# Newton rounds of two reciprocal square roots moved from VectorE to GpSimd in a streaming encoder layer

## The chip, the cores and the metric

The kernel runs on one core of a Trainium2 chip. The metric is the device time of one execution in microseconds (us). The core has five engines that work at the same time and take their own instructions in order: TensorE (PE, matrix products and transposes; PEld are its weight loads), VectorE (DVE), ScalarE (ACT), GpSimd (POOL) and SyncE (SP), which here issues the DMAs. Where an engine needs a result of another one (or, here, where DVE or POOL needs its own earlier result), the instruction waits on a semaphore, and what stands behind it on that engine waits too.

## The reference

One inference step of one hybrid layer for 1024 prompt tokens and 8 x 16 sample tokens, width 1024. The parts that matter here, cut:

```python
h = rmsnorm(x, g_norm)
proj = h @ w_in                                    # 81 groups of 128 columns
r, k, v, w_lr, a_lr, z_a = split(token_shift_mix(proj[..., :SHIFT_COLS]))
kap_h = (k * k_removal).reshape(B, T, 16, 64)
kh_h = kap_h / maximum(norm(kap_h, axis=-1), 1e-12)          # first reciprocal root
y, S = wkv7_scan(wkv0, r_h, w_h, kh_h, a_h, v_h, kt_h)       # recurrence, one state per head
mu = mean(y, -1); var = mean(square(y - mu), -1)
yn = (y - mu) * lax.rsqrt(var + GN_EPS)                      # second reciprocal root
out_a = ((yn * gn_w + gn_b + bonus) * silu(z_a)) @ w_o_a
out_b = (gb * causal_conv3(gc * xb) * silu(z_b)) @ w_o_b
x = x + (sigmoid(g_a) * out_a + sigmoid(g_b) * out_b) @ w_out
x = x + sigmoid(rmsnorm(x, g_ple) @ w_ple_gate) * (p @ w_ple)
y = rmsnorm(x, g_final)
```

## The kernel before

Tokens lie in three blocks: 0 (512 prompt tokens), 1 (the 128 sample tokens) and 2 (the other 512 prompt tokens). The work has three stages. The prologue normalises `x` and transposes it. The recurrence goes through 8 pairs of heads, each with the 3 blocks: 24 steps, named by pair and block, so that `yc4_0` is the `yc` of pair 4, block 0. The last stage multiplies by `w_ob`, `w_oa` and `w_out`, adds the layer's embedding and norms again.

The recurrence is written as seven streams of Python generators. `prep` projects `k`, `r`, `v`, `z` and makes the keys; `scores`, `values` and `inverse` prepare the chunks of 64 tokens; `chain` carries the state `sbd` from chunk to chunk; `tail` makes the output `y`, normalises it per head and writes it to `oa_d`; `conv` is the other branch, whose large matmuls fill gaps. The function `go()` lays these streams into one order on PE: it counts estimated PE time, resumes a stream when the delay that it yielded (`yield 11.0`, in us) has passed, and puts dense matmuls between. That order on PE is fixed. The order on DVE, ACT and POOL isn't written by hand: the tile framework's scheduler lists the instructions by its own estimate of when each can run.

A reciprocal square root is made by `rsqrt`: a seed from the bits of the float (line 134), and three Newton rounds of three instructions (lines 137 to 139), on tiles of 128 partitions by at most 8 columns. It is called

- in `prologue` (5 calls) and in `rstd_rows` for the norms of the last stage (8 calls);
- in `prep` (24 calls, result `nrk`): PE sums squares into `pss`, line 405 copies them to `ssm`, `rsqrt` follows, and ACT spreads the result over 64 columns as `rnb` (line 408). After the products of `v`, PE transposes `rnb` into `prn`, and line 421 scales `k` with it;
- in `tail` (24 calls, result `nry`): the variance `yvr` (lines 705, 706), `rsqrt`, then line 708 multiplies `yc` with it. PE transposes `yc` into `py`, and lines 715, 716 finish the block, which a DMA of SP's queue writes.

Other names that come up: `bdgt` (line 583 on ACT; also line 599 on DVE) and `bdtn` (lines 560, 561 on DVE) are operands of the matmuls that invert a chunk's triangular matrix; `tt`, `tn` (lines 584, 588) are its running inverse; `gt` (line 578) is ACT's copy of one step of it; `xs` (line 643), `vu` (line 649) and `sbd` (line 654) belong to the state's chain; `Spt` (line 638) is POOL's share in it; `thd` (line 362), `zb` (line 768) and `pt` (line 372) are other work of POOL; `wlo...` (line 149) are weight splits.

Of the kernel before, what the change touches and what calls it, by code (L numbers as in the profile page):

```python
# [14 lines left out]
ALU = mybir.AluOpType  # L15
# [56 lines left out]
def _build(nc, tc, I, O, top):  # L72
    V, A, G, PE, SP = nc.vector, nc.scalar, nc.gpsimd, nc.tensor, nc.sync
# [54 lines left out]
        V.tensor_scalar(out=half[:, n, :], in0=par[:, o:o + 8], scalar1=0.5, scalar2=None, op0=ALU.mult)  # L128
    V.tensor_scalar(out=half[:, 3, :], in0=half[:, 2, :], scalar1=-1.0, scalar2=1.0, op0=ALU.mult, op1=ALU.add)

    def rsqrt(x, n, tag):
        y = small.tile([128, 8], F32, tag="nr", name="nr" + tag, bufs=4)[:, :n]
        a = small.tile([128, 8], F32, tag="na", name="na" + tag)[:, :n]
        V.tensor_scalar(out=y.bitcast(I32), in0=x.bitcast(I32), scalar1=-0.5, scalar2=float(0x5F3759DF),
                        op0=ALU.mult, op1=ALU.add)
        for _ in range(3):
            V.tensor_tensor(out=a, in0=y, in1=x, op=ALU.mult)
            V.scalar_tensor_tensor(out=a, in0=a, scalar=-0.5, in1=y, op0=ALU.mult, op1=ALU.mult)
            V.scalar_tensor_tensor(out=y, in0=a, scalar=1.5, in1=y, op0=ALU.add, op1=ALU.mult)
        return y  # L140

    def load_w(src, nm):
# [176 lines left out]
    def load_q(j, q):  # L319
        s = pair(j)  # L320
        if q not in s.w:
            t = {"k": T_K, "r": T_R, "v": T_V, "z": T_ZA}[q]
            s.w[q] = load_w(I["w_in"][t + j], f"p{j}_{t}")
# [17 lines left out]
    def prep(f):  # L341
# [8 lines left out]
        smp, nch, npr, nm = f.smp, f.nch, f.npr, f.nm  # L350
        th = []
        for q, hb in (("d", 0), ("a", 1)):
# [13 lines left out]
                             op0=ALU.mult, op1=ALU.add)  # L366
# [11 lines left out]
        for q, t in (("k", T_K), ("r", T_R), ("v", T_V), ("z", T_ZA)):  # L378
            load_q(j, q)
            if q == "v":  # L380
                yield lambda: S_tail.at >= f.i - 2
            ps = yield from dense_parts(s.w[q], blk, q + nm)
            if ahead:
                load_q(j + 1, q)
            if q == "v":
                x = f.v = tt(wk, "v", "v" + nm, 3, RN)[:, :n]
            elif q == "z":
                x = f.zs = tt(wk, "zs", "zs" + nm, 3, RN)[:, :n]
            else:
                x = tt(st_, "ta", q + nm, TA)[:, :n]  # L390
            mu = (zmu[:, i, j:j + 1] for i in range(3)) if q == "z" else (
                P("mu", t + j), mum[:, t + j:t + j + 1], mus[:, t + j:t + j + 1])
            mixed(ps, t + j, blk, x, *mu, q + nm)
            m[q] = x
            if q == "r":
                x = m["k"]
                yield 4.0

                sq = tt(st_, "ta", "sq" + nm, TA)[:, :n]
                A.activation(sq, x, AF.Square, scale=P("krem", j))  # L400
                pss = psa.tile([128, 512], F32, tag="a", name="pss" + nm)
                for i in range(npr):
                    mm(pss[:, 2 * i:2 * i + 2], sq[:, i * 128:(i + 1) * 128], onesb[:, 0:128:64], start=True, stop=True)
                ssm = small.tile([128, 8], F32, tag="ssm", name="ssm" + nm)
                V.tensor_scalar(out=ssm[:, :2 * npr], in0=pss[:, :2 * npr], scalar1=1e-24, scalar2=None, op0=ALU.max)
                rn = rsqrt(ssm[:, :2 * npr], 2 * npr, "k%d" % npr)
                rnb = tt(st_, "ta", "rnb" + nm, TA)[:, :n]
                A.activation(rnb.rearrange("p (q t) -> p q t", t=64), rn.unsqueeze(2).to_broadcast([128, 2 * npr, 64]),
                             AF.Copy)
            if q == "v":  # L410

                k = m["k"]
                yield 3.0
                prn = psa.tile([128, 512], F32, tag="a", name="prn" + nm)
                for i in range(npr):
                    tr(prn[:, i * 128:(i + 1) * 128], rnb[:, i * 128:(i + 1) * 128], ident)
                kt = tt(st_, "ta", "kt" + nm, TA)[:, :n]
                V.tensor_scalar(out=kt, in0=tha, scalar1=half[:, 2, j:j + 1], scalar2=half[:, 3, j:j + 1],
                                op0=ALU.mult, op1=ALU.add)
                V.tensor_tensor(out=kt, in0=kt, in1=k, op=ALU.mult)  # L420
                V.scalar_tensor_tensor(out=k, in0=k, scalar=P("krem", j), in1=prn[:, :n], op0=ALU.mult, op1=ALU.mult)
                V.scalar_tensor_tensor(out=tha, in0=tha, scalar=1.0, in1=k, op0=ALU.add, op1=ALU.mult)
# [236 lines left out]
    def tail(f):  # L659

        j, s = f.j, f.s
        blk = o, n = f.blk
        smp, nch, npr, nm = f.smp, f.nch, f.npr, f.nm
        nu = 2 * npr
        W = nu * 64
        vu, kbt, pt, scy, yst, bv, zs = f.vu, f.kbt, f.pt, f.scy, f.yst, f.bv, f.zs
        yield 1.0
        yps = psa.tile([128, 4, 2, 64], F32, tag="a", name="y" + nm)[:, :npr]
        for p in range(npr):
            for h, H in enumerate(HS):  # L670
                for e in range(2):
                    mm(yps[HS[e], p, h, :], scy[:, h, p, e, :], vu[:, 2 * p + e, H], start=True, stop=True)
        f.y_done = not smp
        if o + n == 1024:
            for h, H in enumerate(HS):
                SP.dma_start(O["wkv_p"][j, H], sbd[f.st][H, H])
        if smp:
            sst = s.sst
            sso = tt(wk, "ty", "sso" + nm, 2, RN).rearrange("p (s v) -> p s v", v=64)
            for c in range(2):  # L680
                vux = tt(wk, "ty", f"vux{nm}_{c}", 2, RN).rearrange("p (s v) -> p s v", v=128)
                G.tensor_tensor(out=vux, in0=vu[:, c, :].unsqueeze(1).to_broadcast([128, 4, 128]),
                                in1=seq4.unsqueeze(2).to_broadcast([128, 4, 128]), op=ALU.mult)
                yield 1.5
                pS = psc.tile([128, 4, 64], F32, tag="c", name=f"pS{nm}_{c}")
                for h, H in enumerate(HS):
                    mm(pS[H], kbt[:, c, H], vux[:, :, H], start=True, stop=True)
                V.tensor_tensor(out=sso[:, 4 * c:4 * c + 4, :], in0=sst[:, 4 * c:4 * c + 4, :], in1=pS, op=ALU.add)
            f.y_done = True
            V.tensor_tensor(out=sso, in0=sso, in1=pt.unsqueeze(2).to_broadcast([128, 8, 64]), op=ALU.mult)  # L690
            SP.dma_start(O["wkv_s"][j], sso)


        yw = yps.rearrange("p c h v -> p (c h) v")
        y = tt(wk, "ty", "yc" + nm, 2, RN)[:, :W].rearrange("p (u v) -> p u v", v=64)
        ysm = small.tile([128, 8], F32, tag="ysm", name="ysm" + nm)[:, :nu]
        V.tensor_tensor(out=y, in0=yst.rearrange("p c (h v) -> p (c h) v", h=2), in1=yw, op=ALU.add)
        V.tensor_reduce(out=ysm, in_=y, op=ALU.add, axis=AX.X)
        V.tensor_scalar(out=ysm, in0=ysm, scalar1=1.0 / 64, scalar2=None, op0=ALU.mult)
        bcu = lambda x: x.unsqueeze(2).to_broadcast([128, nu, 64])  # L700
        V.tensor_tensor(out=y, in0=y, in1=bcu(ysm), op=ALU.subtract)
        y2 = tt(wk, "ty", "y2" + nm, 2, RN)[:, :W].rearrange("p (u v) -> p u v", v=64)
        A.activation(y2, y, AF.Square)
        yvr = small.tile([128, 8], F32, tag="yvr", name="yvr" + nm)[:, :nu]
        V.tensor_reduce(out=yvr, in_=y2, op=ALU.add, axis=AX.X)
        V.tensor_scalar(out=yvr, in0=yvr, scalar1=1.0 / 64, scalar2=GN_EPS, op0=ALU.mult, op1=ALU.add)
        yrs = rsqrt(yvr, nu, "y%d" % nu)
        V.tensor_tensor(out=y, in0=y, in1=bcu(yrs), op=ALU.mult)
        yf = y.rearrange("p u v -> p (u v)")
        yield 11.0  # L710
        py = psa.tile([128, 512], F32, tag="a", name="py" + nm)
        for i in range(npr):
            tr(py[:, i * 128:(i + 1) * 128], yf[:, i * 128:(i + 1) * 128], ident)
        oa = yf[:, :n]
        V.scalar_tensor_tensor(out=oa, in0=py[:, :n], scalar=P("gnw", j), in1=bv, op0=ALU.mult, op1=ALU.add)
        V.scalar_tensor_tensor(out=oa, in0=oa, scalar=P("gnb", j), in1=zs, op0=ALU.add, op1=ALU.mult)
        SP.dma_start(oa_d[j, :, o:o + n], oa)
# [155 lines left out]
    op = top.enter_context(tc.tile_pool(name="op", bufs=1))  # L873
# [48 lines left out]
    for j in range(KT):  # L922
        w = load_wr(I["w_ob"][j], f"b{j}")
        for blk in BL3:
            o, n = blk
            ps = dense_r(w, obs, blk, f"ob{j}_{o}")
            V.scalar_tensor_tensor(out=ms[j][:, o:o + n], in0=ms[j][:, o:o + n], scalar=1.0, in1=ps,
                                   op0=ALU.add, op1=ALU.mult)
# [11 lines left out]
    for j in range(KT):  # L940
        w = load_wr(I["w_oa"][j], f"a{j}")
        g = gts[j]
        for blk in BL3:
            o, n = blk
# [220 lines left out]
```

## Time and profile before

| | us |
|---|---|
| runs | 1968.08, 1969.87, 1972.9; median 1969.87 |
| the profiled execution, its own time | 1966.13 |
| its span, from the first to the last instruction | 1963.5 |
| PE busy | 1822.7 (93%) |
| DVE busy | 1255.0 (64%) |
| ACT busy | 814.5 (41%) |
| POOL busy | 215.6 (11%) |

The span was recorded in one execution by the profiler. "Busy" is the time in which an engine had an instruction in work; waiting isn't in it. The mean granted clock of PE was 0.984 of full speed.

### The profile page before, as it was taken

What the parts mean: (1) busy time and instruction counts of PE and PEld (TensorE: products, weight loads), DVE (VectorE), ACT (ScalarE), POOL (GpSimd) and SP (SyncE); (2) the same over time, 40 slices, a digit from 0 to 9 for tenths busy, and PEclk for the clock granted to TensorE, in tenths of its full rate; (3) what the DMA queues carried; (4) which work ended last, traced back from release to release, by engine and by line L of the source; (5) the groups of instructions that cost most, each with busy time, mean ns of one, the idle gap of its engine ahead of it and who ended that gap; (6) DMA issues with size and microseconds to landing.
All of it is one profiled execution on the core that took longest, in us unless ns stands there. A gap on an engine that the chain in (4) does not pass through costs nothing. (4 is left out here: it accounts for less than half of the span.)

```text
span 1963.5 us, 37863 instructions
## 1 busy us (share of the span) xinstructions
PE 1822.7 (93%) x15374; PEld 1254.4 (64%) x15374; DVE 1255.0 (64%) x3225; ACT 814.5 (41%) x1877; POOL 215.6 (11%) x333
## 2 busy tenths in 40 slices
PE   4999989989999999999999989889999999999997
PEld 2555666556556556556556556555599677899766
DVE  7477877777687787777887877774223311355665
ACT  6354544544445445445455454443301311322321
POOL 0010121111111111112111111110000011100000
PEclk9999999999999999999999999889999999999999
DMA  6002102101111110201101100022312311243002
GB/s 214 22 23 69 39 14 65 35 28 49 39 40 39 49 40 28 60 29 36 61 28 36 50 8 18 15 69 69 123 42 73 121 44 33 67 123 92 11 29 82
DMA packets 43758, 103.57 MB, mean 53 GB/s; under 512 B 6208, under 2 KB 21440, under 8 KB 43584
## 3 DMA queue, kind: packets, MB, share of 16 engines
q1 hardware_dynamic: 43584, 101.17, 16.2%
q8 instruction: 120, 1.97, 0.4%
q14 instruction: 54, 0.44, 0.1%
HBM read 84.40 MB, written 16.74 MB: 52 GB/s over the span
## 5 line engine op out<-in xcount | busy, mean ns | idle before, releaser
L92 PEld LDWEIGHTS <-whip 128*128 128x128 f16 x1536 | 133.8, 99 | 79.2 <-issue 4.9
L638 POOL TENSOR_SCALAR Spt<-sbd,pt 128x128 f32<-128x128 f32 x128 | 89.8, 702 | 645.1 <-DVE sbd L654 643.8
L92 PEld LDWEIGHTS <-wlop 128*128 128x128 f16 x768 | 75.5, 98 | 61.8 <-issue 2.2
L583 ACT ACTIVATE bdgt<-ig 64x512 f16<-64x512 f32 (+1 forms) x208 | 106.7, 513 | 2.8
L654 DVE SCALAR_TENSOR_TENSOR sbd<-u,pt,Spt 64x64 f32<-64x64 f32 x256 | 72.1, 282 | 52.0 <-PE u L92 44.0
L92 PE MATMUL dB<-hx,whiB 128*128 128x512 f16 (+1 forms) x384 | 91.6, 331 | 3.7 <-ACT sho L236 2.8
L92 PE MATMUL dgb<-hx,whigb 128*128 128x512 f16 (+1 forms) x384 | 91.6, 331 | 2.4 <-ACT whigb L148 1.8
L92 PE MATMUL dzb<-hx,whiZ 128*128 128x512 f16 (+1 forms) x384 | 88.6, 326 | 4.7 <-ACT sho L229 4.7
L644 ACT ACTIVATE yst<-c 64x128 f32<-64x128 f32 x144 | 38.8, 270 | 129.3 <-DVE xs L643 128.1
L92 PE MATMUL dC<-hx,whiC 128*128 128x512 f16 (+1 forms) x384 | 89.9, 327 | 1.5 <-ACT cs L735 1.0
L92 PE MATMUL dv<-hx,whip 128*128 128x512 f16 (+1 forms) x384 | 90.7, 330 | 0.0
L578 ACT ACTIVATE gt<-ig 128x512 f16<-128x512 f32 (+1 forms) x104 | 54.2, 521 | 87.7 <-PE ig L92 87.1
L92 PE MATMUL dk<-hx,whip 128*128 128x512 f16 (+1 forms) x384 | 90.5, 332 | 0.0
L92 PE MATMUL dr<-hx,whip 128*128 128x512 f16 (+1 forms) x384 | 89.0, 326 | 1.4 <-DVE zb L767 1.4
L92 PE MATMUL dz<-hx,whip 128*128 128x512 f16 (+1 forms) x384 | 89.6, 326 | 0.0
L92 PE MATMUL pg<-xn,pg 128*128 128x384 f16 (+1 forms) x576 | 88.9, 309 | 0.0
L92 PE MATMUL dx<-hx,whiX 128*128 128x512 f16 (+1 forms) x384 | 88.3, 326 | 0.5 <-ACT sho L229 0.4
L92 PE MATMUL dga<-hx,whiga 128*128 128x512 f16 (+1 forms) x384 | 86.9, 326 | 0.0
L92 PEld LDWEIGHTS <-pg 128*128 128x128 f16 x768 | 66.3, 99 | 27.1 <-issue 2.4
L649 ACT ACTIVATE vu<-u 64x64 f32<-64x64 f32 x288 | 62.9, 218 | 46.8 <-PE u L92 43.4
L92 PEld LDWEIGHTS u<-xs,tm 128*128 128x128 f32 x288 | 49.9, 191 | 36.8 <-DVE xs L643 21.5
L643 DVE TENSOR_TENSOR xs<-c,vu 64x128 f32<-64x128 f32 x144 | 41.1, 286 | 49.9 <-PE c L92 48.1
(325 smaller groups left out, 4944.1 us busy)
## 6 DMA issues: line engine op xcount, KB each, us to landing
wstp<-i_w_in SPq DMA_DIRECT2D x32, 512.0 KB, 3.6
xt<-i_x SPq DMA_DIRECT2D x9, 512.0 KB, 5.4
ob_d<-zb SPq DMA_DIRECT2D x8, 576.0 KB, 2.9
ostb<-ob_d SPq DMA_DIRECT2D x24, 192.0 KB, 3.0
osta<-oa_d SPq DMA_DIRECT2D x24, 192.0 KB, 2.5
xr<-i_xT SPq DMA_DIRECT2D x8, 576.0 KB, 3.6
wstC<-i_w_in SPq DMA_DIRECT2D x8, 512.0 KB, 3.5
wstX<-i_w_in SPq DMA_DIRECT2D x8, 512.0 KB, 3.5
```

The source lines that it names most:

```text
L92: PE.matmul(out, lhsT, rhs, start=start, stop=stop)
L578: A.activation(Gt, pg, AF.Copy, scale=-1.0)
L583: A.activation(Gb[R, :, R], pg[R], AF.Copy, scale=-1.0)
L638: G.tensor_scalar(out=Spt, in0=S, scalar1=pt[:, c:c + 1], scalar2=None, op0=ALU.mult)
L643: V.tensor_tensor(out=xs[Uh, :], in0=pc[Uh, 0:128], in1=vu[Uh, c, :], op=ALU.add)
L644: A.activation(yst[Vh, p, :], pc[Vh, 0:128], AF.Copy)
L649: A.activation(vu[Uh, c, H], pu[H, H], AF.Copy, scale=-1.0)
L654: V.scalar_tensor_tensor(out=S2[H, H], in0=pu[H, 128 + h * 64:192 + h * 64], scalar=pt[H, c:c + 1], in1=Spt[H, H], op0=ALU.mult, op1=ALU.add)
```

## The change

`rsqrt` gets the engine of its rounds as an argument. The calls in `prep` and `tail` give GpSimd (`G`), the others stay on VectorE. The seed stays on VectorE in all. A round has four instructions instead of three, on either engine, since the two that multiply by a scalar and a tensor at once (SCALAR_TENSOR_TENSOR) are taken apart; the arithmetic is the same.

```diff
-    def rsqrt(x, n, tag):
+    def rsqrt(x, n, tag, E=None):
+        E = E or V
...
         V.tensor_scalar(out=y.bitcast(I32), in0=x.bitcast(I32), scalar1=-0.5, scalar2=float(0x5F3759DF),
                         op0=ALU.mult, op1=ALU.add)
         for _ in range(3):
-            V.tensor_tensor(out=a, in0=y, in1=x, op=ALU.mult)
-            V.scalar_tensor_tensor(out=a, in0=a, scalar=-0.5, in1=y, op0=ALU.mult, op1=ALU.mult)
-            V.scalar_tensor_tensor(out=y, in0=a, scalar=1.5, in1=y, op0=ALU.add, op1=ALU.mult)
+            E.tensor_tensor(out=a, in0=y, in1=x, op=ALU.mult)
+            E.tensor_tensor(out=a, in0=a, in1=y, op=ALU.mult)
+            E.tensor_scalar(out=a, in0=a, scalar1=-0.5, scalar2=1.5, op0=ALU.mult, op1=ALU.add)
+            E.tensor_tensor(out=y, in0=a, in1=y, op=ALU.mult)
         return y
...
-                rn = rsqrt(ssm[:, :2 * npr], 2 * npr, "k%d" % npr)
+                rn = rsqrt(ssm[:, :2 * npr], 2 * npr, "k%d" % npr, G)
...
-        yrs = rsqrt(yvr, nu, "y%d" % nu)
+        yrs = rsqrt(yvr, nu, "y%d" % nu, G)
```

The order on PE in the recurrence is almost untouched, but the scheduler lists DVE, ACT and POOL anew. Behind line 143 the new kernel's line numbers are 2 higher (408 becomes 410, 708 becomes 710), and the seed is line 135. Three places of pair 4 follow.

First place, VectorE around `yc4_0`. Before, 18 rounds' instructions of `yc4_0`'s and `rnb5_0`'s roots stand between the seeds and `yc4_0`; these are the last rows:

```order
L643 TENSOR_TENSOR xs1_135<-c4_1_1_10934,vu4_1_10072 64x128
...
L139 SCALAR_TENSOR_TENSOR nry8_10820<-nay8_10821,nry8_10820 128x8
L139 SCALAR_TENSOR_TENSOR nrk4_10886<-nak4_10887,nrk4_10886 128x8
L708 TENSOR_TENSOR yc4_0_10809<-yc4_0_10809,nry8_10820 128x512
L584 COPY_PREDICATED tt4_2_10616<-cph_99,i134_2_10959 128x512
L747 TENSOR_TENSOR u5_512_10974<-cs5_9667,dx5_512_10716 128x512
```

Now, on VectorE:

```order
L135 TENSOR_SCALAR nry8_10916<-yvr4_0_10913 128x8
L135 TENSOR_SCALAR nrk4_10985<-ssm5_0_10983 128x8
L562 COPY bdtn_128<-tn4_2_10711 64x8x64
L563 COPY bdtn_128<-tn4_2_10711 64x8x64
L645 TENSOR_TENSOR xs1_135<-c4_1_1_11036,vu4_1_10165 64x128
L710 TENSOR_TENSOR yc4_0_10905<-yc4_0_10905,nry8_10916 128x512
L420 TENSOR_SCALAR kt5_0_11345<-tha5_0_10637,half_89 128x512
L586 COPY_PREDICATED tt4_2_10712<-cph_99,i134_2_11061 128x512
```

`yc4_0` comes four rows after its seed. The rounds stand on GpSimd, where those of the two roots alternate; here is the first round, behind a `vux` that was there before:

```order
L684 TENSOR_TENSOR vux4_1_0_11143<-vu4_1_10165,cpk_98 128x512
L138 TENSOR_TENSOR nay8_10917<-nry8_10916,yvr4_0_10913 128x8
L138 TENSOR_TENSOR nak4_10986<-nrk4_10985,ssm5_0_10983 128x8
L139 TENSOR_TENSOR nay8_10917<-nay8_10917,nry8_10916 128x8
L139 TENSOR_TENSOR nak4_10986<-nak4_10986,nrk4_10985 128x8
L140 TENSOR_SCALAR nay8_10917<-nay8_10917 128x8
L140 TENSOR_SCALAR nak4_10986<-nak4_10986 128x8
L141 TENSOR_TENSOR nry8_10916<-nay8_10917,nry8_10916 128x8
L141 TENSOR_TENSOR nrk4_10985<-nak4_10986,nrk4_10985 128x8
```

On ScalarE at the same place, before:

```order
L578 ACTIVATE gt34_2_10947<-ig34_2_10938 128x512
L644 ACTIVATE yst4_1_10760<-c4_1_1_10934 64x128
L583 ACTIVATE bdgt_129<-ig34_2_10938 64x8x64 x2
L408 ACTIVATE rnb5_0_10898<-nrk4_10886 128x512
L649 ACTIVATE vu4_1_10072<-u4_1_1_10955 64x64 x2
```

and now:

```order
L646 ACTIVATE yst4_1_10856<-c4_1_1_11036 64x128
L580 ACTIVATE gt34_2_11049<-ig34_2_11040 128x512
L410 ACTIVATE rnb5_0_11000<-nrk4_10985 128x512
L585 ACTIVATE bdgt_129<-ig34_2_11040 64x8x64
L651 ACTIVATE vu4_1_10165<-u4_1_1_11057 64x64 x2
L585 ACTIVATE bdgt_129<-ig34_2_11040 64x8x64
```

`rnb5_0` has moved ahead of both `bdgt` copies.

Second place, VectorE around `yc4_1`, where a `y` root stands alone. Before:

```order
L599 TENSOR_TENSOR bdgt_129<-loit4_2_11168,ie4_2_11187 64x8x64
L138 SCALAR_TENSOR_TENSOR nay2_11108<-nay2_11108,nry2_11107 128x2
L599 TENSOR_TENSOR bdgt_129<-loit4_2_11168,ie4_2_11187 64x8x64
L139 SCALAR_TENSOR_TENSOR nry2_11107<-nay2_11108,nry2_11107 128x2
L767 SCALAR_TENSOR_TENSOR zb5_10981<-thb5_1024_11224,dzb5_1024_11180 128x128
L708 TENSOR_TENSOR yc4_1_11096<-yc4_1_11096,nry2_11107 128x128
```

and now:

```order
L135 TENSOR_SCALAR nry2_11209<-yvr4_1_11206 128x2
L229 SCALAR_TENSOR_TENSOR v5_0_11281<-dv5_0_11188,mus_83,v5_0_11281 128x511
L710 TENSOR_TENSOR yc4_1_11198<-yc4_1_11198,nry2_11209 128x128
L601 TENSOR_TENSOR bdgt_129<-loit4_2_11273,ie4_2_11292 64x8x64 x2
L769 SCALAR_TENSOR_TENSOR zb5_11083<-thb5_1024_11329,dzb5_1024_11285 128x128
```

The two `bdgt` subtractions that stood ahead of `yc4_1` stand behind it.

Third place, ScalarE around `rnb5_1`, where a `k` root stands alone. Before:

```order
L583 ACTIVATE bdgt_129<-ig25_0_11675 64x8x64 x2
L649 ACTIVATE vu4_2_10846<-u4_2_4_11712 64x64 x2
L408 ACTIVATE rnb5_1_11704<-nrk1_11692 128x128
L148 ACTIVATE whiX6_11757<-wstX6_11755 128x1024
L578 ACTIVATE gt35_0_11774<-ig35_0_11765 128x512
```

and now:

```order
L585 ACTIVATE bdgt_129<-ig25_0_11780 64x8x64 x2
L651 ACTIVATE vu4_2_10945<-u4_2_4_11820 64x64
L410 ACTIVATE rnb5_1_11812<-nrk1_11797 128x128
L651 ACTIVATE vu4_2_10945<-u4_2_4_11820 64x64
L150 ACTIVATE whiX6_11865<-wstX6_11863 128x1024
```

`rnb5_1` has moved between the two `vu4_2` copies of one chunk.

## Rows read from the trace of the kernel before

**Rows 1.** The page, busy time, share of the span and instructions of each engine.
```profile
PE 1822.7 (93%) x15374; PEld 1254.4 (64%) x15374; DVE 1255.0 (64%) x3225; ACT 814.5 (41%) x1877; POOL 215.6 (11%) x333
```

**Rows 2.** Windows: stretch, length, busy PE PEld DVE ACT POOL, clock, DMA, GB/s.
```profile
60.00:1360.00 1300.00, 1206.55 (x11565) 755.07 (x11563) 970.18 (x2592) 624.25 (x1508) 186.12 (x294) 0.99 0.12 38
849.00:1003.00 154.00, 142.85 (x1417) 91.15 (x1417) 119.77 (x325) 76.87 (x188) 23.77 (x37) 1.00 0.12 40
```

**Rows 3.** What PE waited for: us in total, times, longest us.
```profile
PE u L92 <- DVE xs L643: 12.7, 10, 2.2
...
PE prq L246 <- DVE nrq L139: 3.1, 3, 2.3
PE py L96 <- DVE yc L708: 2.8, 3, 1.7
```

**Rows 4.** Groups by form on DVE: count | busy us, mean ns | idle before.
```profile
L137 DVE TENSOR_TENSOR nay<-nry,yvr 128x8 f32<-128x8 f32 x48 | 7.8, 162 | 0.7
```

**Rows 5.** Groups by form on POOL.
```profile
L638 POOL TENSOR_SCALAR Spt<-sbd,pt 128x128 f32<-128x128 f32 x128 | 89.8, 702 | 645.1 <-DVE sbd L654 643.8 <-POOL pb L368 0.2
...
L362 POOL TENSOR_SCALAR thd<-thd 128x512 f32<-128x512 f32 x16 | 24.3, 1519 | 100.0 <-ACT thd L359 86.9 <-DVE sbd L654 13.0
L768 POOL TENSOR_TENSOR zb<-zb,cv 128x512 f32<-128x512 f32 x16 | 23.7, 1482 | 79.1 <-DVE zb L767 79.1
...
L372 POOL COPY pt<-pb 128x8 f32<-128x8 f32 x24 | 6.6, 276 | 28.1 <-ACT pb L370 27.8
L362 POOL TENSOR_SCALAR thd<-thd 128x128 f32<-128x128 f32 x8 | 6.2, 772 | 26.5 <-ACT thd L359 26.5
...
L768 POOL TENSOR_TENSOR zb<-zb,cv 128x128 f32<-128x128 f32 x8 | 3.6, 456 | 44.5 <-DVE zb L767 37.1 <-DVE nry L139 7.4
```

**Rows 6.** Timeline of POOL: start us, duration us, instruction.
```profile
304.58 0.21 POOL L618 MEMSET sbd<- 128x128 f32 x1 [0.93 <-PE ie L92]
304.88 0.72 POOL L638 TENSOR_SCALAR Spt<-sbd,pt 128x128 f32<-128x128 f32 x1
```

**Rows 7.** Timeline of DVE, first place.
```profile
851.16 0.49 DVE L134 TENSOR_SCALAR nry<-yvr 128x8 int32<-128x8 int32 x1
851.57 0.16 DVE L134 TENSOR_SCALAR nrk<-ssm 128x8 int32<-128x8 int32 x1
...
854.18 0.69 DVE L708 TENSOR_TENSOR yc<-yc,nry 128x512 f32<-128x512 f32 x1
```

**Rows 8.** Timeline of ACT, first place.
```profile
854.20 1.21 ACT L583 ACTIVATE bdgt<-ig 64x512 f16<-64x512 f32 x2
855.44 0.63 ACT L408 ACTIVATE rnb<-nrk 128x512 f32<-128x512 f32 x1
```

**Rows 9.** Timeline of PE, first place.
```profile
855.53 0.40 PE L92 MATMUL i<-tn,bdgt 128*128 128x64 f16 x8
```

**Rows 10.** Timelines of DVE and PE, second place.
```profile
872.71 0.17 DVE L134 TENSOR_SCALAR nry<-yvr 128x2 int32<-128x2 int32 x1
...
874.70 0.67 DVE L599 TENSOR_TENSOR bdgt<-loit,ie 64x512 f16<-64x512 f16 x1
...
877.99 0.40 PE L92 MATMUL if<-tn,bdgt 128*128 128x64 f16 x8
```

**Rows 11.** Timelines of DVE, ACT and PE, third place.
```profile
909.82 0.17 DVE L134 TENSOR_SCALAR nrk<-ssm 128x2 int32<-128x2 int32 x1
...
911.78 0.31 ACT L408 ACTIVATE rnb<-nrk 128x128 f32<-128x128 f32 x1
...
912.72 0.47 PE L92 MATMUL u<-vu,kbt 128*128 128x128 f32 x2
```

**Rows 12.** The chain that ended last, at the last tail: start us, us, what.
```profile
1356.19 0.18 DVE nry L134
...
1359.25 0.70 DVE yc L708
```

**Rows 13.** One tile's instructions, `bdtn` on DVE: duration ns min/median/max.
```profile
L560 DVE COPY bdtn<-tn x104: 177/280/1350, 117.8 to 1313.6; 64x512 f16<-64x512 f16 x80, 64x128 f16<-64x128 f16 x24
```

## Prediction

> **What bounds the kernel now.** I read the head of the page first: TensorE (PE) is busy for 1822.7 of 1963.5 us, VectorE (DVE) for 1255.0, GpSimd (POOL) for 215.6 [rows 1]. Then the windows: in the recurrence (60 to 1360 us) DVE is busy 970.18 of 1300 us, and in one period of it (849 to 1003 us, one pair of heads, three blocks of tokens) PE is busy 142.85 of 154 us, DVE 119.77 [rows 2]. So PE bounds the recurrence, and it leaves 154 - 142.85 = 11.15 us per period unused. The list of waits shows that these are small waits for DVE and ScalarE (ACT): the largest, `u<-xs`, is 12.7 us in all in ten pieces, `py<-yc` 2.8 us in three [rows 3]. PE takes its work in the fixed order of `go()`, so whatever comes late by more than its slack stops PE. The question is therefore not how much work DVE loses but whether a result that PE needs comes later.
>
> **What the change takes from DVE.** A round is three dependent instructions of about 0.16 us [rows 4], with issue about 0.2 us from start to start: a reciprocal root of nine costs 1.8 us of DVE. 48 of them (24 `k`, 24 `y`) are 86 us of 970, in an engine that is a quarter idle. By itself that is worth a little: PE waits for DVE with perhaps half of its 11.15 us per period.
>
> **What a chain costs on POOL.** No row shows such a small arithmetic operation there, so I bound it. TENSOR_TENSOR takes 1482 ns for 512 and 456 ns for 128 columns [rows 5]: 2.67 ns a column, so 456 - 120 x 2.67 = 136 ns for 8. The nearest real row is the 128x8 COPY `pt`, 276 ns. I take 0.20 us between them. TENSOR_SCALAR with immediate operands, the form of line 140 of the new kernel, takes 1519 ns for 512 and 772 ns for 128 columns [rows 5]: 1.95 ns a column, 540 ns for 8; I take 0.50 us, near to that row, with 0.14 (a TENSOR_TENSOR) and 0.70 us (`Spt`) as ends. A POOL instruction that needs the one before it starts late: the memset of `sbd` ends at 304.79 us, the `Spt` that reads it starts at 304.88 us [rows 6], 0.09 us. All twelve depend in this way. One chain alone is 9 x (0.20 + 0.09) + 3 x (0.50 + 0.09) = 4.4 us, and with a like 0.1 us for each crossing between engines **4.6 us** from the end of the seed (line 134, which stays on DVE) to the reader. By the low ends it is 12 x 0.23 + 0.2 = 3.0 us, by the high ones 9 x 0.366 + 3 x 0.79 + 0.2 = 5.9 us. On DVE it is 1.8 us.
>
> **What stands behind it.** The order printed above decides it: the scheduler moved the readers forward, as if the chain were short. `yc` (line 708) follows its seed on DVE after one or a few instructions, and `rnb` (line 408) stands on ACT ahead of work that PE needs soon. Both engines take instructions in order, so they stand still until POOL is done, with everything behind. I work out three places of one period; the others have the same form.
>
> Place A, `yc4_0` and `rnb5_0`. Seeds start at 851.16 and 851.57 us and `yc` at 854.18 [rows 7]. On POOL the two chains alternate, so one runs in the other's gaps: 9 x 0.29 + 3 x 0.89 = 5.3 us, from 851.75 to 857.05 us. DVE resumes at 857.1, 2.9 us late. ACT's `rnb` goes from 855.44 to about 857.3 us, and two `bdgt` copies, which ran from 854.20, now stand behind it [rows 8], with `vu` between them: 857.3 + 0.63 + 0.6 + 0.45 + 0.6 = 859.6 us. PE reads `bdgt` at 855.53 us [rows 9]: **4.1 us late**. DVE's own 2.9 us lie inside that, since PE then comes to DVE's next result 4.1 us later too.
>
> Place B, `yc4_1`, a `y` alone. The seed starts at 872.71 and ends at 872.88 us [rows 10]; 4.6 us later, at 877.5, `yc` runs (0.3 us), and the two L599 of 0.67 us that stood ahead of it [rows 10] now come behind: 877.5 + 0.3 + 1.3 = 879.1 us. PE's `if` reads them at 877.99 us [rows 10]: **1.2 us late**.
>
> Place C, `rnb5_1`, a `k` alone. The seed ends at 909.99 us, so `rnb` moves from 911.78 to 914.6 us, and one of the two `vu` copies, now behind it, ends at 915.2 us. PE's `u` that reads it started at 912.72 us [rows 11]: **2.5 us late**. The relief counts here: DVE goes on without its 1.8 us, but PE waits for ACT.
>
> Block 2 of the period has one more of B's form and one more of C's (there `rnb` holds up a `gt` copy). A period: 4.1 + 2 x 1.2 + 2 x 2.5 = 11.5 us; eight periods 92 us. Not all stays. Each time that PE stands, DVE and ACT catch up, and a later small wait of PE shrinks; PE has 11.15 us of them per period. If 40% is taken back so, 0.6 x 92 = **55 us** remain. That factor is my choice, between 0.5 (half of those 11.15 us goes) and 1.
>
> **What else moves.** In the calls that stay on DVE a round has four instructions, so a call is 3 x 0.2 = 0.6 us longer. The first prologue call, the three waits of PE for `nrq` (3.1 us) [rows 3] and the last call lie on the path: 5 x 0.6 = 3 us. The others lie under dense matmuls; uncovered, the other eight would cost 5 us. The tail of the last block sets when `oa_d` is written and when the loads behind it in SP's queue start: seed 1356.19, `yc` 1359.25 us [rows 12], with a weight split between, which now comes after. New: 1356.37 + 4.6 = 1361.0, **1.7 us later**. POOL's own late work costs nothing that I can see: the `Spt` that comes up to 3 us late is needed a chunk later, some 6 us on. DMAs are neither added nor removed.
>
> **Sum.** 1966.1 (the profiled execution: span 1963.5 and 2.6 around it) + 55 + 3 + 2 = 2026 us. The median of the runs lies 3.7 us above the profiled one, so 2026 to 2030; I say **2028 us**. Low prices: A 1.6, B 0, C 0.9, a period 3.4, eight times 0.6: 16 us, 1985 us. High prices: 6.6 + 2 x 2.5 + 2 x 3.8 = 19.2 a period, 92 us at 0.6 and 154 us at 1: 2063 to 2125 us. Within 0.3%, about 6 us, a measurement of this kernel can't tell a change from none.
>
> **Rivals.** First, the two engines hinder each other at SBUF. For it: the 64x512 `bdtn` copy, whose median is 280 ns, once took 1350 ns [rows 13]. Against it: in a `y` chain DVE mostly stands still and can't be in the way. If it holds, the high prices do, and DVE's later work is slowed, so less is taken back: 0.8 x 8 x 19.2 = 123 us, 2094 us. The Trainium skill (SBUF — State Buffer, Who interferes with whom) says that a DVE copy in a two-port mode, or a DVE instruction with two SBUF inputs, and a reading POOL instruction exclude each other for a whole instruction. The long `bdtn` copy agrees with that rule. Chance 0.18.
>
> Second, the other side: POOL does the small operations at the low prices or under. Then a chain (3.0 us) is no longer than what passes today from seed to `yc` (3.0 us at A, 3.9 at B), the waits at `yc` vanish, and DVE's freed 86 us tell. If a quarter of PE's unused time goes, 8 x 11.15 / 4 = 22 us less half of that for `rnb`, plus the 3 us of the longer calls: 1966 - 11 + 3 = 1958 us. It decides at about 3 us a chain. Against it: line 140's form has no row under 772 ns. Chance 0.07.
>
> Third, the lateness is taken back entirely, since PE's order leaves some 2 us between `yc` and `py` (it waited there in 3 of 24 calls [rows 3]) and more ahead of `prn` (none of its waits): 1969 us, no change. Against it: the stall doesn't come from `py` or `prn`, but from what stands behind the readers in DVE's and ACT's queues. Chance 0.08.
>
> **Numbers.** The forecast has 0.67, the rivals 0.18, 0.07 and 0.08. Slower by over 0.3%: 0.67 + 0.18 = 0.85; same 0.08; faster 0.07. The range from 1985 (low prices) to 2085 (short of the first rival's centre) leaves out the no-change and faster cases and part of the first rival, about 0.2.
>
> **What would show it.** Right: POOL busy grows by 576 x 0.275 = 158 us (48 chains of 12, by the mid prices); the chain takes 4 to 5 us; among waits, DVE `yc` for POOL `nry` and ACT `rnb` for POOL `nrk` of 2 to 4 us each, together over 60 us; PE waits for `bdgt`, `vu` and `sbd` grow; a period becomes some 7 us longer, and PE's busy time stays. Wrong: a chain under 3 us; waits of DVE and ACT as forecast, yet periods as long as before (then the factor 0.6 is wrong); or a longer time in the stage behind 1404 us, of which I price only 1 or 2 us.

## Result: slower by 4.1%, and the profile after

Four runs of the changed kernel took 2042.14 to 2054.51 us, median **2050.61**; four of the kernel before 1964.53 to 1972.9, median 1968.97. The ratio is 1.0409 (95% interval 1.037 to 1.0449). The forecast was 2028 us in a range from 1985 to 2085.

The head of the page of the changed kernel, against [rows 1]:

```profile
PE 1846.5 (90%) x15374; PEld 1261.8 (62%) x15374; DVE 1205.5 (59%) x2832; ACT 813.0 (40%) x1877; POOL 347.0 (17%) x909
```

The span is 2049.3 us, 85.8 more than before. PE runs the same 15374 instructions, yet is busy for 23.8 us more; the other 62.0 us is time in which PE stands. DVE is relieved by 49.5 us, POOL has 131.4 us more. The next view is the windows, with the columns of [rows 2]; the first line is the recurrence, which now ends some 79 us later, and the second the period from `yc4_0` on, which took 154.3 us before:

```profile
60.00:1439.00 1379.00, 1227.99 (x11569) 762.05 (x11567) 916.93 (x2163) 623.88 (x1510) 310.48 (x870) 0.97 0.11 36
910.50:1075.00 164.50, 148.11 (x1418) 92.39 (x1417) 113.75 (x271) 77.22 (x187) 38.50 (x110) 0.97 0.12 37
```

PE stands in the recurrence for 1379 - 1227.99 = 151.0 us, before for 1300 - 1206.55 = 93.5. So nearly all of the loss arises there: 57.5 us of standing and 21.4 us of busier time. The period is 10 us longer; here about half of that is PE's busy time (148.11 against some 143), over the whole recurrence about a quarter.

The waits (us in total, times, longest) name the two readers:

```profile
ACT rnb L410 <- POOL nrk L141: 68.7, 24, 6.0
DVE yc L710 <- POOL nry L141: 62.8, 24, 4.2
...
PE u L92 <- DVE xs L645: 18.3, 14, 2.2
PE u L92 <- ACT vu L651: 18.1, 15, 5.3
PE i L92 <- ACT gt L580: 17.0, 10, 3.8
...
PE i L92 <- ACT bdgt L585: 10.1, 7, 2.0
...
PE py L96 <- DVE yc L710: 4.7, 2, 2.5
```

and before, for the three of ACT:

```profile
PE u L92 <- ACT vu L649: 5.9, 10, 1.3
...
PE i L92 <- ACT gt L578: 2.5, 4, 0.7
...
PE i L92 <- ACT bdgt L583: 1.1, 3, 0.5
```

All 24 `rnb` and all 24 `yc` wait for POOL, 131.5 us together. PE hardly waits for the roots themselves: for `yc` at `py` it is 4.7 us, and no wait for `rnb` is among its waits at all. It waits for `vu`, `gt` and `bdgt`, ordinary work of ACT that stands behind `rnb` (45.2 us together, 9.5 before), and for `xs` of DVE (18.3 us, 12.7 before [rows 3]).

The first place of the prediction, by the timelines of DVE, POOL, ACT and PE (start us, us, engine, instruction; in brackets how long the engine stood before it and for whom), against [rows 7 to 9]:

```profile
910.94 0.49 DVE L135 TENSOR_SCALAR nry<-yvr 128x8 int32<-128x8 int32 x1
911.35 0.16 DVE L135 TENSOR_SCALAR nrk<-ssm 128x8 int32<-128x8 int32 x1
...
911.51 0.25 POOL L138 TENSOR_TENSOR nay<-nry,yvr 128x8 f32<-128x8 f32 x1
...
914.91 0.19 POOL L140 TENSOR_SCALAR nay<-nay 128x8 f32<-128x8 f32 x1
915.07 0.19 POOL L140 TENSOR_SCALAR nak<-nak 128x8 f32<-128x8 f32 x1
915.23 0.20 POOL L141 TENSOR_TENSOR nry<-nay,nry 128x8 f32<-128x8 f32 x1
915.38 0.20 POOL L141 TENSOR_TENSOR nrk<-nak,nrk 128x8 f32<-128x8 f32 x1
915.46 0.69 DVE L710 TENSOR_TENSOR yc<-yc,nry 128x512 f32<-128x512 f32 x1 [2.94 <-POOL nry L141]
915.62 0.63 ACT L410 ACTIVATE rnb<-nrk 128x512 f32<-128x512 f32 x1 [1.52 <-POOL nrk L141]
...
917.09 0.59 ACT L585 ACTIVATE bdgt<-ig 64x512 f16<-64x512 f32 x1
...
917.74 0.41 PE L92 MATMUL i<-tn,bdgt 128*128 128x64 f16 x8 [1.90 <-ACT bdgt L585]
```

It goes as the prediction has it: both engines stand until POOL is done, the second `bdgt` comes behind `rnb` and `vu`, and PE waits for it. Only the pair of chains is shorter, 4.07 us (911.51 to 915.58) instead of 5.3.

The second and third place (`yc4_1`, `rnb5_1`) end so on PE:

```profile
939.25 0.41 PE L92 MATMUL if<-tn,bdgt 128*128 128x64 f16 x8 [0.48 <-DVE bdgt L601]
...
975.41 0.49 PE L92 MATMUL u<-vu,kbt 128*128 128x128 f32 x2 [1.23 <-ACT vu L651]
```

The costliest place is the `k` root of block 2, of which the prediction said only that "there `rnb` holds up a `gt` copy":

```profile
1017.32 1.64 POOL L640 TENSOR_SCALAR Spt<-sbd,pt 128x128 f32<-128x128 f32 x1
1017.33 1.25 DVE L151 SCALAR_TENSOR_TENSOR wloZ<-wstZ,whiZ 128x1024 f16<-128x1024 f32 x1 [0.60 <-ACT whiZ L150]
...
1020.29 0.63 ACT L410 ACTIVATE rnb<-nrk 128x512 f32<-128x512 f32 x1 [3.00 <-POOL nrk L141]
1020.94 0.60 ACT L737 ACTIVATE cs<-dC 128x512 f32<-128x512 f32 x1
1021.44 0.27 ACT L580 ACTIVATE gt<-ig 128x128 f16<-128x128 f32 x1
...
1021.76 0.27 PE L92 MATMUL i<-gt,bdtn 128*128 128x64 f16 x2 [3.77 <-ACT gt L580]
```

The same matmul before:

```profile
956.23 0.22 PE L92 MATMUL i<-gt,bdtn 128*128 128x64 f16 x2 [0.69 <-ACT gt L578]
```

POOL's own `Spt` stands in the middle of this chain, and takes 1.64 us there. The chain becomes 5.0 us long; `gt`, a copy of 0.27 us, comes behind `rnb` and `cs`; PE stands for 3.77 us, where it stood for 0.69. Then something follows that the prediction doesn't have. In the windows right behind this wait and behind the same wait one pair later, the number behind POOL's is PE's granted clock:

```profile
1021.80:1027.50 5.70, 5.70 (x19) 2.47 (x19) 2.82 (x7) 1.03 (x5) 0.00 (x0) 0.50 0.00 0
...
1186.40:1192.00 5.60, 5.48 (x35) 3.04 (x35) 3.40 (x10) 3.09 (x11) 0.03 (x1) 1.00 0.02 3
```

And PE's timeline at both:

```profile
1021.84 1.04 PE L92 MATMUL dv<-hx,whip 128*128 128x512 f16 x2
...
1186.52 0.22 PE L92 MATMUL i<-gt,bdtn 128*128 128x64 f16 x2 [3.77 <-ACT gt L580]
1186.58 0.59 PE L92 MATMUL dv<-hx,whip 128*128 128x512 f16 x2
```

After the first wait of 3.77 us PE got a granted clock of 0.50, its level of 1.2 GHz, and the pair of `dv` matmuls took 1.04 us; after the second one, as long, the clock stayed at 1.00 (2.4 GHz) and the same pair took 0.59 us. So a wait can cost PE a second time, in slower matmuls, and doesn't always.

### The profile page after: what moved, and what is told of

Read it like the earlier page. It is cut to its first block, busy times and chain, and to the rows that moved or that the text cites. A ratio compares the mean times of both kernels' runs of the same rounds, so it can differ in the third digit from the quotient of the medians.

```text
span 2049.3 us, 38005 instructions
## 1 busy us (share of the span) xinstructions
PE 1846.5 (90%) x15374; PEld 1261.8 (62%) x15374; DVE 1205.5 (59%) x2832; ACT 813.0 (40%) x1877; POOL 347.0 (17%) x909
## 4 chain that ended last, share of the span: by engine, by line
PE 63%; DVE 15%; ACT 8%; POOL 6%; issue 5%; DMA 3%; POOLq 0%; SPq 0%; DVEq 0%; ACTq 0%
PE ob L92 5%; PE dga L92 5%; PE oc L92 5%; PE dz L92 4%; PE oa L92 4%; PE dk L92 4%; PE dC L92 3%; PE pg L92 3%; PE dB L92 3%; PE dr L92 3%; PE dgb L92 3%; PE u L92 3%; PE dv L92 3%; PE dx L92 2%; PE dzb L92 2%
## 5 line engine op out<-in xcount | busy, mean ns | idle before, releaser
L949 POOL TENSOR_TENSOR ms<-ms,gt 128x384 f32<-128x384 f32 x24 | 31.6, 1318 | 336.7 <-DVE gt L948 336.7
L586 DVE CAST_PREDICATED tt<-cph,i 128x512 f16<-128x512 uint16 (+1 forms) x104 | 61.8, 594 | 31.9 <-PE i L92 30.5
```

The source lines that it names most:

```text
L586: V.copy_predicated(out=Tt, mask=bc(lvt[:, b, :]).bitcast(U16), data=p1)
L949: G.tensor_tensor(out=ms[j][:, o:o + n], in0=ms[j][:, o:o + n], in1=g[:, o:o + n], op=ALU.add)
```

## Experiments

The median, the ratio to the kernel before, run on the same chip in the same group of runs, with its interval, and from the profiled execution PE's busy time and the rest of the span, in which PE stands. The median of the kernel before was 1968.49 us in the group of `split_v`, `shadow`, `k_only` and `y_only`, 1968.51 in that of `rounds1`, `rounds5`, `late_c` and `readers_g`, and 1967.15 in that of `late_b`, `kg`, `v_rnbg` and `v_late`:

| kernel | us | ratio (95%) | PE busy | PE stands |
|---|---|---|---|---|
| before | 1968.97 | | 1822.7 | 140.8 |
| the change | 2050.61 | 1.0409 (1.037, 1.0449) | 1846.5 | 202.8 |
| split_v | 1978.62 | 1.0052 (1.0034, 1.007) | 1829.1 | 150.8 |
| shadow | 1969.02 | 1.001 (0.9996, 1.0023) | 1824.3 | 144.6 |
| k_only | 2032.38 | 1.0317 (1.0294, 1.0341) | 1846.3 | 184.0 |
| y_only | 2000.3 | 1.0161 (1.0145, 1.0176) | 1831.8 | 165.1 |
| rounds1 | 1971.55 | 1.002 (1.0007, 1.0033) | 1825.0 | 145.0 |
| rounds5 | 2132.58 | 1.0843 (1.0811, 1.0875) | 1880.2 | 246.5 |
| late_c | 1992.79 | 1.0122 (1.0094, 1.015) | 1834.4 | 156.7 |
| late_b | 1976.22 | 1.0049 (1.0029, 1.0068) | 1825.7 | 150.1 |
| readers_g | 1981.08 | 1.0071 (1.0049, 1.0093) | 1827.0 | 151.4 |
| kg | 1962.24 | 0.9972 (0.9962, 0.9982) | 1821.0 | 141.7 |
| v_rnbg | 1965.85 | 0.9996 (0.9985, 1.0007) | 1819.7 | 143.7 |
| v_late | 1960.5 | 0.9969 (0.9953, 0.9984) | 1818.1 | 140.3 |

The theory to be tested is that of the forecast, called the queue theory below: the readers `yc` and `rnb` stand at the head of DVE's and ACT's queues while POOL works, and what PE needs stands behind them.

**split_v: is it the instruction count?** All rounds on VectorE again, in four instructions:

```diff
-                rn = rsqrt(ssm[:, :2 * npr], 2 * npr, "k%d" % npr, G)
+                rn = rsqrt(ssm[:, :2 * npr], 2 * npr, "k%d" % npr)
...
-        yrs = rsqrt(yvr, nu, "y%d" % nu, G)
+        yrs = rsqrt(yvr, nu, "y%d" % nu)
```

> All rounds stay on VectorE, but have four instructions as in the change. Queue theory (readers placed early stop VectorE and ScalarE while GpSimd works): no reader waits for another engine, so only the longer calls count: 61 calls by 0.6 us of VectorE, of which some 5 us lie on the path: 1970 to 1976 us. Rival (the new listing of VectorE and ScalarE, or the two extra instructions, cost the time by themselves): 2000 us or more.

Measured 1978.62 us, 10 more than before and 3 above what was expected. Taking the rounds apart costs a little where they stay on VectorE; it doesn't explain 82 us.

**shadow: is it contention?** The kernel before, with a chain on GpSimd beside each root that nobody reads (`one8` is a tile of ones):

```diff
+        if G is not None:
...
+            G.tensor_copy(gy, x)
+            for _ in range(3):
+                G.tensor_tensor(out=ga, in0=gy, in1=one8[:, :n], op=ALU.mult)
+                G.tensor_tensor(out=ga, in0=ga, in1=one8[:, :n], op=ALU.mult)
+                G.tensor_scalar(out=ga, in0=ga, scalar1=-0.5, scalar2=1.5, op0=ALU.mult, op1=ALU.add)
+                G.tensor_tensor(out=gy, in0=ga, in1=one8[:, :n], op=ALU.mult)
         for _ in range(3):
             V.tensor_tensor(out=a, in0=y, in1=x, op=ALU.mult)
```

> Before, with its three-instruction rounds on VectorE, and beside each of the 48 calls a chain of 13 dependent operations of the same shapes on GpSimd (a copy of the input, then three rounds of four with a tile of ones), which nobody reads. Output unchanged. Queue theory: GpSimd is as busy as in the change (some 130 us more than before) but no engine waits for it, so the time stays within 1% of before, 1965 to 1985 us. Rival (GpSimd hinders VectorE at the memory): the same operations on GpSimd lengthen VectorE's instructions, and at least half of the 82 us comes back: 2010 us or more.

The head of its page:

```profile
PE 1824.3 (93%) x15374; PEld 1255.4 (64%) x15374; DVE 1256.3 (64%) x3226; ACT 813.0 (41%) x1877; POOL 365.6 (19%) x957
```

POOL is busier than in the change, DVE's busy time is that of before within 1.3 us, and the time is 1969.02 us, that of before. GpSimd's small operations by themselves cost nothing: as the cause of the loss the first rival falls. That VectorE's work lengthens a chain on GpSimd is not tested by this run, since nobody waits for its chain.

**k_only and y_only: which reader?** Each gives `G` to one of the two calls only.

> Only the 24 roots of the keys on GpSimd; those of the outputs stay on VectorE, in four instructions. Queue theory: ScalarE's waits at rnb stay (over 50 us in all), VectorE's at yc vanish. The steps of tensor engine's lateness that follow from ScalarE (bdgt, vu and gt behind rnb: 2.1, 1.4 and 3.1 us of a period) stay, and with them most of the clock's loss: 2010 to 2040 us. A rival in which the wait at yc is what costs: under 1990 us.

> Only the 24 roots of the outputs on GpSimd; those of the keys stay on VectorE, in four instructions. Queue theory: VectorE's waits at yc stay (about 60 us in all), ScalarE's at rnb vanish. They cost the tensor engine less, 0.7 us at the second place and one or two elsewhere: 1980 to 2005 us. If each of the two halves cost the same, both would come to about 2010 us.

Of the waits of `k_only`:

```profile
ACT rnb L410 <- POOL nrk L141: 63.8, 24, 6.0
...
PE i L92 <- ACT gt L580: 16.3, 6, 3.8
PE u L92 <- ACT vu L651: 15.5, 15, 2.4
```

and of `y_only`:

```profile
DVE yc L710 <- POOL nry L141: 57.4, 24, 4.2
ACT rnb L410 <- DVE nrk L141: 23.9, 20, 5.2
...
PE u L92 <- ACT vu L651: 5.9, 10, 1.3
...
PE i L92 <- ACT gt L580: 0.4, 1, 0.4
```

The keys' half costs 64 us (2032.38 less 1968.49, the median before in this group of runs), the outputs' half 32 (2000.3 less 1968.49), though the reader's engine stands for about as long in both (63.8 and 57.4 us). The sum of the halves is 96; each holds the other's rounds in four instructions on VectorE, which together is `split_v`'s 10. 96 - 10 = 86 us, near the change's 82: the two causes add up. What stands behind `rnb` on ACT (`gt`, `vu`, `bdgt`) is dearer than what stands behind `yc` on DVE: PE's waits for `gt` and `vu` are 31.8 us in `k_only` and 6.3 in `y_only`.

**rounds1 and rounds5: does the cost follow the chain's length?**

```diff
-        for _ in range(3):
+        for _ in range(1 if E is G else 3):
```

and with 5 in place of 1.

> The change with one Newton round on GpSimd instead of three in the 48 calls (the output is less exact; the calls that stay on VectorE keep three). A chain is four dependent operations, some 1.3 us, against 1.8 us on VectorE before and 3.7 to 4.2 us in the change. Queue theory: the cost follows the chain's length, so most of it goes: 1965 to 1990 us. Rival (the crossing between engines, or the new order of the queues whatever the chain's length, is what costs): 2020 us or more.

> The change with five rounds on GpSimd instead of three in the 48 calls (two rounds more that alter nothing in the result). A chain is 20 dependent operations, 2.5 us longer than in the change. Queue theory: each of some five late places of a period comes another 2.5 us later, 12 us per period and 8 periods, 0.6 to 1 of it stays, and the clock falls more often: 2115 to 2180 us. Rival (a fixed cost per crossing): 2050 to 2070 us.

The readers' waits with one round:

```profile
ACT rnb L410 <- POOL nrk L141: 36.7, 20, 5.1
DVE yc L710 <- POOL nry L141: 20.9, 24, 1.9
```

and with five:

```profile
ACT rnb L410 <- POOL nrk L141: 106.6, 24, 7.9
DVE yc L710 <- POOL nry L141: 106.4, 24, 5.6
```

One, three and five rounds: 1971.55, 2050.61 and 2132.58 us, 39.5 and 41.0 us per round on the two steps. The cost is the chain's length, not a fixed price of crossing engines. With one round the readers still stand for 57.6 us, yet the time is only 0.2% above before: short waits of a reader cost PE little. DVE has lost 51 us of work there, and no gain from it shows; the readers' waits may hide one.

**late_c and late_b: is it the readers' place?** The roots stay on GpSimd, twelve operations each; the readers are written later and ordered behind the last instruction of their engine until then (`behind` keeps the closure until `go()` has laid so many us of PE work; 4.0 and 9.0 in `late_c`, 5.0 and 8.0 in `late_b`):

```diff
-                A.activation(rnb.rearrange("p (q t) -> p q t", t=64), rn.unsqueeze(2).to_broadcast([128, 2 * npr, 64]),
-                             AF.Copy)
+                behind("A", 4.0, lambda: A.activation(rnb.rearrange("p (q t) -> p q t", t=64),
+                                                     rn.unsqueeze(2).to_broadcast([128, 2 * npr, 64]), AF.Copy))
...
-        V.tensor_tensor(out=y, in0=y, in1=bcu(yrs), op=ALU.mult)
+        behind("V", 9.0, lambda: V.tensor_tensor(out=y, in0=y, in1=bcu(yrs), op=ALU.mult))
```

> The change, all 12 operations on GpSimd, but rnb and yc are written into the program later, 4 and 9 us of estimated tensor time behind where they stood, and ordered behind the last instruction of ScalarE or VectorE that was written until then. So six rows or more stand between seed and yc instead of one to five, and rnb stands two to five rows later on ScalarE. Tensor order as in the change but for a few places. Queue theory: what PE needs soon now stands ahead of the waiting reader, so the waits of VectorE and ScalarE for GpSimd fall under 50 us from 131 and the time to 1970 to 2005 us. Rival (the roots themselves come too late for py and prn): 2030 us or more, with PE's waits for yc and rnb grown.

> As late_c, but with the shifts at 5 and 8 us: yc stands four to nine rows behind its seed instead of six to twelve, rnb as late or later. In late_c the waits at yc and rnb were gone and PE waited 25 us for yc at py. Queue theory: yc may stand too early (others wait behind it) or too late (py waits); an earlier place takes some of the 25 us from py and brings back part of VectorE's 63 us of waits: 1980 to 1995 us. If all that is left in late_c came from yc at py: 1970 to 1978 us.

PE's order is that of the change but for a few places. The waits of `late_c`:

```profile
ACT rnb L421 <- POOL nrk L152: 31.8, 14, 4.8
...
PE py L107 <- DVE yc L721: 25.0, 15, 3.3
DVE yc L721 <- POOL nry L152: 9.0, 6, 3.4
```

and of `late_b`:

```profile
DVE yc L721 <- POOL nry L152: 24.0, 19, 3.5
ACT rnb L421 <- POOL nrk L152: 21.5, 8, 4.6
...
PE py L107 <- DVE yc L721: 8.6, 7, 2.5
```

The same work on the same engines, with the readers a few rows later, takes 58 and 74 of the 82 us away (2050.61 less 1992.79 and less 1976.22). In `late_c` `yc` stands too late: PE waits 25 us for it at `py`. In `late_b`, with `yc` between the two, this wait is 8.6 us, VectorE's wait at `yc` 24.0 us. Its time lies below the range expected of it, and in that of the other case, in which all that was left in `late_c` came from `yc` at `py`; since `late_b` moves `rnb` too, how much each shift gave stays open.

**readers_g: no reader in DVE's and ACT's queues at all.**

```diff
-                A.activation(rnb.rearrange("p (q t) -> p q t", t=64), rn.unsqueeze(2).to_broadcast([128, 2 * npr, 64]),
-                             AF.Copy)
+                G.tensor_copy(rnb.rearrange("p (q t) -> p q t", t=64), rn.unsqueeze(2).to_broadcast([128, 2 * npr, 64]))
...
-        V.tensor_tensor(out=y, in0=y, in1=bcu(yrs), op=ALU.mult)
+        G.tensor_tensor(out=y, in0=y, in1=bcu(yrs), op=ALU.mult)
```

> The change with both readers on GpSimd too (the product yc by a GpSimd multiplication, the spread rnb by a GpSimd copy), so that no instruction of VectorE or ScalarE stands in its queue waiting for a root; the chain from seed to the reader's end becomes longer by 0.7 to 1 us. Queue theory: VectorE's and ScalarE's waits for the roots vanish; PE comes to wait for py in more than two of 24 calls (the slack there is 0.1 to 4.4 us): 1970 to 2005 us. Rival (the length of the chain is on the path by itself): 2060 us or more.

```profile
PE py L96 <- POOL yc L709: 13.2, 8, 4.0
```

PE waits for no other reader of a root in this kernel. The way from the seed to the reader's end is longer than in the change, POOL has the more work, and yet 70 of the 82 us are gone.

**kg, v_rnbg and v_late: is there a gain?** `kg` takes the keys' roots and `rnb` to GpSimd and leaves everything else as before (three-instruction rounds on VectorE); `v_rnbg` moves only `rnb`; `v_late` is the kernel before with `behind("A", 4.0, ...)` for `rnb` and no other edit.

> The keys' roots on GpSimd with their reader rnb on GpSimd too (a copy), everything else as in the kernel before: three-instruction rounds on VectorE for the outputs' roots and the other 13 calls. Tensor order as before. Queue theory: no engine stands waiting for a root, VectorE loses some 43 us of work, ScalarE 13 us and its 14 us of waits at rnb; if relief of these engines is worth anything to the tensor engine it shows here: 1955 to 1968 us. Rival (relief is worth nothing, or rnb comes too late for prn): 1968 to 1985 us.

> The kernel before with nothing changed but rnb: a GpSimd copy instead of ScalarE's; the roots stay on VectorE. Tensor order as before. It takes away ScalarE's 14 us of waits at rnb and 13 us of work. Queue theory: the same head of ScalarE's queue that costs 64 us in the change costs a little already here, so 1960 to 1968 us; a rival in which it is hidden now: 1968 us.

> The kernel before with rnb written into the program 4 us of estimated tensor time later and ordered behind ScalarE's last instruction until then; nothing else changed, tensor order as before. Queue theory: ScalarE's 14 us of waits at rnb fall under 5 us; 1960 to 1968 us. Rival (hidden now): 1968 us.

`kg` takes 1962.24 us, 0.28% less than before; `v_late` 1960.5, 0.31% less, with every root on VectorE. Both intervals leave out 1, but the gains are small. A gain like `kg`'s needs no relief of VectorE, since `v_late` has as much without it. In the profiled executions `v_late` differs from before in PE's busy time, 4.6 us, and not in its standing; one execution each is too little to settle where the 6 us lie. ACT's wait at `rnb`, 14.0 us before, is 6.9 in `v_late`, more than the expected 5. `v_rnbg`, which takes `rnb` off ACT altogether, is no change (1965.85 us, within the range expected of it): its `rnb` waits 63.0 us for DVE at the head of POOL's queue. That this is why it gains nothing was not tested. So that the small gain of `v_late` comes from `rnb` no longer standing in front of ACT's work is not shown.

## Why the prediction was right, and what its size left out

**What bounds, and where the loss arises.** Right. PE bounds the recurrence, no run shows a gain that needs the relief of DVE (`rounds1`, `kg` beside `v_late`), and nearly all of the loss lies between 60 and 1439 us. The relief is smaller than was said: DVE's busy time fell by 49.5 us, while the 86 us of the forecast are counted from start to start and leave out the fourth instruction of a round in the 13 calls that stay.

**The chain on POOL.** Forecast 4.6 us with 3.0 and 5.9 as ends; the median is 4.1 us for `k` and 3.6 for `y`, worked out over the 24 calls each from the end of the seed to the end of the last round. The term that was off is line 140: 0.50 us was taken from the nearest row, and it took 0.19 to 0.25, like a TENSOR_TENSOR. The chain of `y` is so below the 4 to 5 us that were named as a sign of being right. POOL's busy time grew by 131 us, not 158. An operation that waits for its own predecessor starts 0.28 us after that one's start, where 0.29 was worked out.

**The places.** The mechanism was right at each, the prices too high at three: PE was forecast late by 4.1, 1.2 and 2.5 us, and matched row by row with the trace before it came 2.1, 0.7 and 1.4 us later there; at the `gt` of block 2 it was 3.1 us where 2.5 stood. The second place of B's form, priced at 1.2, shows no step. Together 7.2 us a period, where 11.5 was forecast. Of that, about three quarters stayed (PE stands in the period for 16.4 us, before for 11.15), where 0.6 was chosen. The two errors cancel in part: 0.6 x 11.5 = 6.9 was forecast, 5.2 measured in this period. Eight such periods would be 42 us; that PE stands for 57.5 us more over the whole recurrence, near the 55 of the forecast, is in part luck. The loss isn't even, as eight equal periods would have it: the first `yc` already starts 17.8 us late (246.47 us, before 228.67), `yc4_0` 61.3 (915.46, before 854.18 [rows 7]), the last one 78.6 (1437.83, before 1359.25 [rows 12]). Outside the recurrence the forecast was 3 us for the longer calls and 1.7 for the last tail: PE enters the recurrence 3.2 us late, and some 4 us arise behind it. Of the waits of PE that were to grow, those for `bdgt` and `vu` did; those for `sbd` did not (8.6 us before, 7.6 now).

**The step that failed in size** is the sum's silence on PE's clock. Of the 85.8 us, 62.0 are standing; the forecast has 60 (55 + 3 + 2). The other 23.8 us is PE's busy time, which the prediction said would stay. The mean granted clock fell from 0.984 to 0.974; over the spans, (1 - 0.974) x 2049.3 = 53 us of full clock are missing where (1 - 0.984) x 1963.5 = 31 were before. That is 22 us more, an estimate (it counts standing time too) that comes near the 23.8. The matmuls that take longer stand behind waits, as at 1021.8 us. The other kernels show the same pairing: `rounds5` stands 105.7 us more than before and is busy 57.5 more, `k_only` 43.2 and 23.6, `y_only` 24.3 and 9.1. With 0.4 us of busy time per us of standing, a ratio taken from these results (it lies between 0.37 and 0.55 in them) that none of the rows of before gives, the forecast would have been 2052. The mechanism was right, and so nearly was the sum of the waits; what was missing is what waits cost PE in clock.

**The rivals.** Contention fell as the main cause (`shadow`; in the change the instructions that DVE had before too took 2.0 us more in all). It has a share at single places: POOL's `Spt`, 0.60 us in the median, took 1.64 us beside DVE's `wloZ` in the `k` chain at 1017.32 us, and also at 855.58 and 1182.08 us. With this 1.0 us, `rnb` and `gt` come later too. `Spt` took up to 1.68 us before as well, but there no root's chain ran on POOL. The rule of the Trainium skill (SBUF — State Buffer, Who interferes with whom), that a DVE instruction with two inputs in SBUF contends with a reading POOL instruction, agrees with these rows of `Spt` beside `wloZ`; here POOL took longer, not DVE (`wloZ` 1.25 us, 1.23 in the median). The cheap chain fell: it took 3.6 to 4.1 us in the median, and `rounds1` shows that even a shorter one brings nothing. The hidden one was right in one thing, that `py` and `prn` have slack, and fell because of what stands behind the readers, as the prediction argued.

## What to carry to other kernels

Before work is moved to an idle engine, look at who reads its result, on which engine, and what stands behind that reader in its queue: here the slow producer cost little by being slow (in `readers_g`, 13 us above before), and most by an early reader that stopped everything behind it. Give the reader to the slow engine too, or order it behind what the bounding engine needs soon; that took 70 and 74 of 82 us back. Where the bounding engine is TensorE, a wait can be paid for once more in matmuls at the lower clock, so that a sum of waits alone came out too small here.

## What was unexpected in the hardware

Two dependent chains that alternate on POOL run faster than the sum: 24 operations in 4.07 us, one every 0.17 us, most of them recorded as 0.20 us long, against one every 0.28 us for a chain alone (934.34 to 937.58 us for the twelve of `yc4_1`). A TENSOR_SCALAR with two immediate operands on 2 or 8 columns takes 0.19 to 0.25 us in the mean on POOL, though one with a single immediate on 128 columns took 0.77 [rows 5]. And waits of PE of nearly the same length (3.72 to 3.77 us) for `gt`, at the same place of four pairs, were followed by 1.2 GHz twice (from 860.0 and 1021.8 us, in the first case for a part of the window) and by 2.4 GHz twice (from 698.4 and 1186.4 us). Here are the two windows that are not shown above:

```profile
698.42:704.00 5.58, 5.58 (x35) 3.08 (x35) 4.17 (x12) 2.74 (x10) 0.60 (x1) 1.00 0.30 94
860.02:865.60 5.58, 5.58 (x25) 2.64 (x25) 2.82 (x7) 1.76 (x8) 0.00 (x0) 0.69 0.00 0
```

What decides it stays open. The Trainium skill (TensorE: Matmul & The Clock Gate, HAM oscillation — how this bites in real kernels) describes a kernel whose waits for DMA take the clock down each time; here the waits are for ScalarE, and the trace agrees at 860.0 and 1021.8 us and not at 698.4 and 1186.4 us.
